# Seven block products for eight in the input projection of a convolution layer (fp32 network, one Trainium2 core)

## The chip, the cores and the metric

The kernel runs on one core of a Trainium2 chip. The metric is device microseconds of one execution; the time of a version is the median of several runs. The engines are TensorE (PE in the profile, with PEld for its weight loads), VectorE (DVE), ScalarE (ACT), GpSimd (POOL) and SyncE (SP), whose queue issues the DMAs.

## The reference

The network passes 1024 latent tokens of 1024 features, and 256 context tokens, through four layers: a pooling mixer, neighbourhood attention, a short gated convolution, and a pooling mixer again. The change is in the third. With `h` the RMS-normed, scaled and shifted tokens, it computes

```python
bg, cg, v, g = jnp.split(h @ w_in, 4, axis=-1)          # w_in: 1024 x 4096
y = bg * _dwconv3(cg * v, conv_w, conv_b)               # 3 taps over tokens, per feature
x = x + gate[:, None] * ((y * jax.nn.silu(g)) @ w_out)  # w_out: 1024 x 1024
```

All of it is fp32.

## The kernel before, in words

Activations lie transposed: features on the 128 partitions, tokens along the free dimension, in eight feature tiles (`KT`) and two token halves of 512 (`HALF`, called `ch` 0 and 1). A product keeps fp32 accuracy with fp32r matmuls: each operand is split into a high part (ACT, a copy to fp32r, L79) and a low part (DVE or POOL, source minus high part, L80), and `mm3` (to L117) issues three matmuls of 128x128 by 128x512 per contraction tile: high-high (L115), high-low (L116), low-high (L117). So one output tile of one token half (`gemm`, L133) is 8 x 3 = 24 matmuls into one PSUM bank; there are 8 banks.

The order of TensorE's instructions is the order of the program. On DVE, ACT, POOL and SP a planner orders the instructions ahead of time, by priority (place in the program) among those that its own timing takes to be ready; at run time each engine's queue is then strictly in that order. Tiles come from pools with a fixed number of buffers: `a` (`slot`, 33 tiles of 4 KB per partition) for activations, `raw` (3) for weights as loaded, `whi` and `wlo` (3 each) for their parts, `t2` (3 tiles of 2 KB) for temporaries. A tile's buffer is free when its last reader is done.

In `rest` (L1303) the attention layer's output projection (`out_proj`, L342) runs for token half 0 and then for half 1, with old residual rows loaded by `x1_rows` (L1019). Each finished half gives its sums of squares; `norm_later` (L281) hangs the normalisation on later gemms: the token sums on TensorE (L240), a chain of small DVE steps to the reciprocal root (L251 to L271), its spread over partitions on TensorE (L278), and `modulate_k` per feature tile (multiply by the spread in PSUM, L305; scale and shift for the high part, L306; the same again in fp32, L308 or L310; low part, L311).

`conv_in` (L1352) then loops over the 8 feature tiles of the output. For each it loads four weight tiles of 128x1024 (blocks cg, v, g, bg; `weight`, L82) and makes eight gemms, four blocks by two token halves. For the first tile the four gemms on half 0 come before those on half 1. ACT copies cg out of PSUM (L1369) and takes SiLU of g (L1373), DVE multiplies v by cg into `z` (L1371), then come three taps (L1390 to L1392), the product with bg straight from PSUM (L1395), with SiLU(g) on POOL (L1396), and the split for the next projection (L1398). `weight` also moves a background queue on: 24 reductions for the last layer's adaLN vector, each a 512 KB load into `raw` (L162) and one DVE reduction of 1024 columns (L166). Next is `out_proj` for `conv_out`, over the eight tiles of y, in SBUF.

## Time and profile before

| what | value |
|---|---|
| time, three runs | 1942.8, 1946.7 and 1949.32 us, median 1946.7 |
| profiled execution | 1943.86 us, span 1942.1 us |
| mean granted TensorE clock | 0.985 of full |
| TensorE busy | 1864.4 us (96%), 9936 matmuls |
| DVE, ACT, POOL busy | 1095.8 us (56%), 729.1 us (38%), 571.1 us (29%) |
| DMA | 274.21 MB, mean 141 GB/s |
| matmuls of `mm3` with loaded weights (L115) | x2160, 380 ns mean of one |

A matmul's recorded duration covers its whole passage and overlaps the next one's; the distance between two starts is what one costs in a row of them. Busy shares are averages over stages with different limits, so a stage is read from windows of its own. A releaser in brackets is the engine whose work ended the idle time named before it. All queues are in order, so an instruction that waits holds up what is behind it.

### The profile page before, as it was taken

What the parts mean: (1) busy time and instruction counts of PE and PEld (TensorE: products, weight loads), DVE (VectorE), ACT (ScalarE), POOL (GpSimd) and SP (SyncE); (2) the same over time, 40 slices, a digit from 0 to 9 for tenths busy, and PEclk for the clock granted to TensorE, in tenths of its full rate; (3) what the DMA queues carried; (4) which work ended last, traced back from release to release, by engine and by line L of the source; (5) the groups of instructions that cost most, each with busy time, mean ns of one, the idle gap of its engine ahead of it and who ended that gap; (6) DMA issues with size and microseconds to landing.
All of it is one profiled execution on the core that took longest, in us unless ns stands there. A gap on an engine that the chain in (4) does not pass through costs nothing.

```text
span 1942.1 us, 27112 instructions
## 1 busy us (share of the span) xinstructions
PE 1864.4 (96%) x9936; PEld 1604.0 (83%) x9936; DVE 1095.8 (56%) x2251; ACT 729.1 (38%) x1401; POOL 571.1 (29%) x552
## 2 busy tenths in 40 slices
PE   7888899999999999999998999999999999999997
PEld 4677778889998889999997877788888887888887
DVE  7989977256431066667666678544323346432627
ACT  3332215245122155666666555222212225322422
POOL 4645312652110033444433443100000024433120
PEclk9989999999999999999999999999999999999999
DMA  6233351554763466676677646443111165011234
GB/s 253 76 108 99 114 190 60 188 161 142 247 231 108 144 186 191 193 210 188 197 200 216 188 154 221 128 129 118 44 55 44 55 184 179 2 49 49 72 122 153
DMA packets 126960, 274.21 MB, mean 141 GB/s; under 512 B 12874, under 2 KB 48458, under 8 KB 126828
## 3 DMA queue, kind: packets, MB, share of 16 engines
q1 hardware_dynamic: 126828, 272.49, 44.9%
q8 instruction: 78, 1.28, 0.3%
q14 instruction: 54, 0.44, 0.1%
HBM read 218.63 MB, written 53.81 MB: 140 GB/s over the span
## 4 chain that ended last, share of the span: by engine, by line
PE 76%; DVE 12%; DMA 6%; issue 3%; POOL 2%; ACT 1%; SPq 0%; DVEq 0%; POOLq 0%; ACTq 0%
PE mm L117 22%; PE mm L115 21%; PE mm L116 21%; DVE junk L166 4%; PE T L1211 3%; PE O L1237 2%; PE O L1236 2%; DMA raw<-in_ada 2%; PE S L1154 1%; DVE S L455 1%; PE S L1155 1%; POOL S L455 1%; DMA a<-in_xT 1%; PE SC L1157 1%; PE SC L1156 1%
## 5 line engine op out<-in xcount | busy, mean ns | idle before, releaser
L115 PE MATMUL mm<-a,whi 128*128 128x512 f32 (+2 forms) x2160 | 819.9, 380 | 22.3 <-DVE U L418 10.0
L116 PE MATMUL mm<-a,whi 128*128 128x512 f32 (+2 forms) x2149 | 804.3, 374 | 10.9 <-DVE a L80 8.5
L117 PE MATMUL mm<-a,wlo 128*128 128x512 f32 (+2 forms) x2160 | 807.1, 374 | 3.5 <-POOL wlo L80 2.4
L115 PEld LDWEIGHTS mm<-a,whi 128*128 128x128 f32 x2160 | 411.5, 191 | 94.7 <-DVE U L418 11.3
L116 PEld LDWEIGHTS mm<-a,whi 128*128 128x128 f32 x2149 | 409.4, 190 | 81.0 <-DVE a L80 10.1
L117 PEld LDWEIGHTS mm<-a,wlo 128*128 128x128 f32 x2160 | 410.8, 190 | 77.9 <-POOL wlo L80 3.7
L80 POOL TENSOR_TENSOR wlo<-raw,whi 128x256 fp32r<-128x256 f32 (+2 forms) x150 | 191.0, 1288 | 382.5 <-ACT whi L79 341.9
L79 ACT ACTIVATE whi<-raw 128x1024 fp32r<-128x1024 f32 (+2 forms) x237 | 170.9, 738 | 352.1 <-PE mm L116 273.6
L166 DVE CUSTOM_DVE_ANT_0 junk<-raw,sil_x,vec 128x1024 bf16<-128x1024 f32 x86 | 117.9, 1371 | 94.4 <-DMA raw<-in_ada 94.1
L80 DVE TENSOR_TENSOR wlo<-raw,whi 128x1024 fp32r<-128x1024 f32 (+1 forms) x87 | 107.6, 1238 | 112.7 <-ACT whi L79 111.2
L1190 POOL TENSOR_SCALAR pr<-pr,rsum 128x640 f32<-128x640 f32 (+1 forms) x128 | 99.8, 779 | 238.8 <-DVE rsum L1189 188.2
L115 PE MATMUL mm<-a,a 128*128 128x512 f32 (+2 forms) x280 | 97.5, 348 | 7.4 <-ACT a L698 6.3
L1181 ACT ACTIVATE pr<-lg,nmx 128x640 f32<-128x640 f32 (+1 forms) x128 | 102.3, 799 | 2.6 <-DVE nmx L1171 1.6
L224 POOL TENSOR_TENSOR a<-a,a 128x512 f32<-128x512 f32 x42 | 59.9, 1425 | 144.2 <-ACT a L223 138.0
L116 PE MATMUL mm<-a,a 128*128 128x512 f32 (+2 forms) x275 | 95.8, 348 | 4.9 <-DVE a L702 4.9
L117 PE MATMUL mm<-a,a 128*128 128x512 f32 (+2 forms) x280 | 96.4, 344 | 0.5 <-DVE a L80 0.5
L1169 DVE TENSOR_SCALAR_CACHE_REDUCE lg<-SC 128x256 f32<-128x256 f32 x128 | 54.2, 423 | 72.9 <-PE SC L1157 72.8
L1220 DVE TENSOR_TENSOR ptlo<-T,pthi 128x512 fp32r<-128x512 f32 x128 | 88.2, 689 | 10.6 <-ACT pthi L1215 8.6
L1236 PE MATMUL O<-pthi,a 128*128 128x256 f32 x352 | 89.0, 286 | 3.2 <-ACT pthi L1215 3.2
L1237 PE MATMUL O<-ptlo,a 128*128 128x256 f32 x352 | 89.6, 289 | 1.1 <-DVE ptlo L1220 0.6
L1215 ACT ACTIVATE pthi<-T 128x512 fp32r<-128x512 f32 x128 | 76.4, 597 | 20.6 <-PE T L1211 19.5
L1211 PE MATMUL T<-ident,pr 128*128 128x128 f32 x512 | 77.6, 274 | 0.0
(182 smaller groups left out, 2495.0 us busy)
## 6 DMA issues: line engine op xcount, KB each, us to landing
raw<-in_ada SPq DMA_DIRECT2D x86, 512.0 KB
raw<-in_pool_out SPq DMA_DIRECT2D x32, 512.0 KB
raw<-in_conv_in SPq DMA_DIRECT2D x32, 512.0 KB
raw<-in_pool_in SPq DMA_DIRECT2D x27, 512.0 KB
x<-a SPq DMA_DIRECT2D x48, 256.0 KB
raw<-in_na_in SPq DMA_DIRECT2D x24, 512.0 KB
a<-dk SPq DMA_DIRECT2D x48, 256.0 KB
dv<-v SPq DMA_DIRECT2D x40, 256.0 KB
```

The costliest lines, as they stand in the source:

```text
L79: self.nc.scalar.activation(hi, src, AF.Copy)
L80: (lo_engine or self.nc.vector).tensor_tensor(lo, src, hi.bitcast(F32), op=ALU.subtract)
L115: t.matmul(ps, wh, hh, start=(begin and k == ks[0]), stop=False)
L116: t.matmul(ps, wh, hl, start=False, stop=False)
L117: t.matmul(ps, wl, hh, start=False, stop=(end and k == ks[-1]))
L166: nc.vector.tensor_tensor_reduce(out=junk[:], in0=raw[:], in1=self.sil[c][:], scale=1.0, scalar=self.vec[:, b:b + 1], op0=ALU.mult, op1=AL ...
L1181: nc.scalar.activation(pr[:, :L + CTX], lg[:, :L + CTX], AF.Exp, bias=nm[:], scale=-1.0, accum_out=sm[:])
L1190: nc.gpsimd.tensor_scalar(pr[:, :L], pr[:, :L], rs[:], 1.0, op0=ALU.mult, op1=ALU.mult)
L1211: nc.tensor.transpose(T[:, (s - b0) * P:(s - b0 + 1) * P], pr[:, o:o + P], self.ident[:])
L1220: nc.vector.tensor_tensor(lv, tv, hv.bitcast(F32), op=ALU.subtract)
L1236: nc.tensor.matmul(ops[:], v, hi[:, s, :], start=(n == 0), stop=False)
L1237: nc.tensor.matmul(ops[:], v, lo[:, s, :], start=False, stop=(n == len(seq) - 1))
```

## The change

Two weight tiles (128 output features each) form a pair: the z pair (cg, v) and the y pair (g, bg) of one feature tile, 16 pairs. In each, the weights are a 2x2 of blocks A (output tile by half of the contraction, four contraction tiles each), the tokens a 2x2 of blocks B (half of the contraction by token half). Eight block products of 12 matmuls become seven, with sums of weight blocks S1 to S4 and of token blocks T1 to T4 (`TERMS`). The products of a pair share three PSUM banks a, b, c: a takes products 1 and 2, b takes 6, 7 and 4, c takes 5 and 3; each bank is read in between and then added to again (`start` only for the first). The outputs are put together by DVE additions and ACT copies (`seven_after`).

The sums S are made per pair, on DVE for the first three pairs and on POOL from the fourth, where POOL also makes the low parts for products 1, 3 and 5. T1 to T4 and B22 are made once, in `conv_in`, from the kept fp32 tiles `x0` and `x1` of the two halves (`modulate_k` with `keep` works in place). The first three pairs are interleaved, so that their products 1 and 2, which need token half 0 alone, come first. Weight parts are made three products ahead. The adaLN reductions come one to every third product, from the fourth pair on.

The blocks B and T hold 28 of the 33 tiles of `a`, so seven of the eight tiles of y go to DRAM (`dyc`) and come back before `conv_out` (`conv_y`). `out_proj` takes the eighth last: for its first two output tiles it multiplies the other seven first (`late`). The second weight tile of a pair is loaded into `a`, the first into `raw`; `t2` has four buffers, and the pools of this stage (`pg`) and of the pooling layer (`pu`) are opened in turn.

```diff
-    def modulate_k(self, x, rs, l, c, k, hi, lo, n, pool=None, act=False):
+    def modulate_k(self, x, rs, l, c, k, hi, lo, n, pool=None, act=False, keep=False):
 ...
+        xh = x if keep else self.pt.tile([P, HALF], F32, tag="t2", name=self.nm("xh"), bufs=self.t2)[:, :n]
 ...
+            begun = {}
             for k in range(KT):
-                Wk = next(W)
+                if late is not None and group is groups[0] and k == 0:
+                    begun = {n: (next(W), self.bank()) for n in range(2)}
+                    for Wk, ps in begun.values():
+                        self.mm3(ps[:], self.wk(Wk), lambda q: y[group[0]][q], [q for q in order if q != late], end=False)
+                Wk = begun[k][0] if k in begun else next(W)
                 for ch in group:
                     g = self.gate(l, "c" if ch == "c" else "x")
                     old = xold(ch, k)
-                    ps = self.gemm(Wk, y, ch, ks.get((ch, k), order))
+                    if k in begun:
+                        ps = begun[k][1][:]
+                        self.mm3(ps, self.wk(Wk), lambda q: y[ch][q], (late,), begin=False)
+                        self.tick()
+                    else:
+                        ps = self.gemm(Wk, y, ch, ks.get((ch, k), order))
 ...
+        last = self.conv_in(h, x32, st)
         self.finish_background()
         h = {}
-        for ch, xn, st in self.out_proj(i["conv_out"], y, 2, ((0,), (1,)), self.old_from(self.x2), self.x3):
+        for ch, xn, st in self.out_proj(i["conv_out"], self.conv_y(last), 2, ((0,), (1,)), self.old_from(self.x2), self.x3, late=KT - 1):
 ...
+    TERMS = {1: ("A11", "B11"), 2: ("A12", "B21"), 3: ("S4", "B22"), 4: ("A22", "T4"), 5: ("S1", "T1"),
+             6: ("S2", "T2"), 7: ("S3", "T3")}
+    H4 = KT // 2
 ...
+            a, b, op = {"S1": ("A21", "A22", ALU.add), "S2": ("S1", "A11", ALU.subtract),
+                        "S3": ("A11", "A21", ALU.subtract), "S4": ("A12", "S2", ALU.subtract)}[name]
+            a, b = self.seven_block(pair, a), self.seven_block(pair, b)
+            t = self.pt.tile([P, HALF], F32, tag="t2", name=self.nm("s"), bufs=self.t2)
+            (self.nc.gpsimd if pair["pool"] else self.nc.vector).tensor_tensor(t[:], a, b, op=op)
+            pair["sums"][name] = t[:]
 ...
+    def seven_weight(self, pair, n):
+
+        src = self.seven_block(pair, self.TERMS[n][0])
+        self.ring = not self.ring
+        t = self.pw.tile([P, 2, HALF], F32R, tag="whi" if self.ring else "wlo", name=self.nm("wp"))
+        on_pool = pair["pool"] and n in (1, 3, 5)
+        self.split(t[:, 0], t[:, 1], src, self.nc.gpsimd if on_pool else None)
+        pair["parts"][n] = t
 ...
+    def seven_product(self, pair, n, T):
+        nc = self.nc
+        bank = "abc"[{1: 0, 2: 0, 6: 1, 7: 1, 4: 1, 5: 2, 3: 2}[n]]
+        first = n in (1, 6, 5)
+        if first:
+            pair[bank] = self.bank()
+        ps = pair[bank][:]
+        t = pair["parts"].pop(n)
+        B = T[self.TERMS[n][1]]
+        for q in range(self.H4):
+            s = slice(q * P, (q + 1) * P)
+            for i, (w, x) in enumerate(((0, 0), (0, 1), (1, 0))):
+                nc.tensor.matmul(ps, t[:, w, s], B[q][x], start=first and q == 0 and i == 0,
+                                 stop=q == self.H4 - 1 and i == 2, skip_group_check=True)
 ...
+        if n == 1:
+            pair["xu"] = self.pg.tile([P, 2, HALF], F32, tag="g", name=self.nm("xu"))
+            nc.scalar.activation(pair["xu"][:, 0], a[:], AF.Copy)
+        elif n == 2:
+            put(1, 0, a[:])
+        elif n == 6:
+            nc.vector.tensor_tensor(pair["xu"][:, 1], b[:], pair["xu"][:, 0], op=ALU.add)
+        elif n == 5:
+            if "ux" in pair:
+                u = pair["ux"][:, 1]
+                nc.vector.tensor_tensor(u, c[:], u, op=ALU.add)
+                put(2, 1, u)
+            else:
+                pair["ux"] = self.pg.tile([P, 2, HALF], F32, tag="g", name=self.nm("ux"))
+                nc.scalar.activation(pair["ux"][:, 0], c[:], AF.Copy)
+        elif n == 3:
+            u = pair["xu"][:, 1]
+            nc.vector.tensor_tensor(u, c[:], u, op=ALU.add)
+            put(1, 1, u)
+        elif n == 7:
+            before = "ux" in pair
+            if not before:
+                pair["ux"] = self.pg.tile([P, 2, HALF], F32, tag="g", name=self.nm("ux"))
+            u = pair["ux"]
+            nc.vector.tensor_tensor(u[:, 1], b[:], pair["xu"][:, 0], op=ALU.add)
+            if before:
+                nc.vector.tensor_tensor(u[:, 1], u[:, 1], u[:, 0], op=ALU.add)
+                put(2, 1, u[:, 1])
+        elif n == 4:
+            x = pair["xu"][:, 0]
+            nc.vector.tensor_tensor(x, b[:], x, op=ALU.add)
+            put(2, 0, x)
 ...
+        for j, (p, n) in enumerate(order):
+            while done < min(j + ahead + 1, len(order)):
+                q, m = order[done]
+                self.seven_weight(pairs[q], m)
+                done += 1
+            for f in hooks.get(j, ()):
+                f()
+            self.seven_product(pairs[p], n, T)
+            self.seven_after(pairs[p], n)
 ...
+                t = self.slot([P, 2, HALF], F32R)
+                nc.sync.dma_start(t[:].bitcast(F32), self.dyc[k][ch].bitcast(F32))
 ...
+        def first():
+            for k in range(H4):
+                self.modulate_k(x1[k], got[1], 2, "x", k, None, None, HALF, act=k % 2, keep=True)
+                sub(x0[k], x1[k], x0[k], False)
+                parts("T1", k, x0[k], k % 2)
+
+        def second():
+            for k in range(H4, KT):
+                self.modulate_k(x1[k], got[1], 2, "x", k, *parts("B22", k, None, None), HALF, k % 2, act=k % 2, keep=True)
+
+        def third():
+            for k in range(H4):
+                sub(x0[k], x1[k + H4], x0[k], k % 2)
+                parts("T2", k, x0[k], k % 2 == 0)
+            for k in range(H4):
+                sub(x1[k], x1[k + H4], x1[k], k % 2)
+                parts("T3", k, x1[k], k % 2 == 0)
+            for k in range(H4):
+                sub(x0[k + H4], x0[k + H4], x0[k], k % 2)
+                parts("T4", k, x0[k + H4], k % 2 == 0)
 ...
+        E = 3
+        order = [(p, 1) for p in range(E)] + [(p, 2) for p in range(E)]
+        for p in range(E):
+            order += [(p, n) for n in (5, 6, 3, 7)]
+            if p:
+                order.insert(-3, (p - 1, 4))
+        for p in range(E, len(pairs)):
+            end = p == len(pairs) - 1
+            steps = [(p, n) for n in ((1, 6, 2, 7, 5, 4, 3) if end else (1, 6, 5, 2, 7, 3, 4))]
+            if p == E:
+                steps.insert(1, (E - 1, 4))
+            order += steps
+        for p in pairs:
+            p["pool"] = True
+        for p in range(E):
+            pairs[p]["pool"] = False
+        hooks = {1: [tokens], 3: [spread, first], 4: [second], 5: [third]}
+        self.bg = [self.ada_all(3, (0, 1, 2))]
+        self.bg_rate = 0
+        for j in range(7 * E + 6, 7 * len(pairs) - 14, 3):
+            hooks.setdefault(j, []).append(lambda: self.background(1))
+        self.seven_run(pairs, T, order, hooks)
 ...
+                nc.vector.tensor_tensor(z[0][:, 1 + ch * HALF:1 + (ch + 1) * HALF], cs[1, ch], cs[2, ch], op=ALU.mult)
 ...
+            if ("g", ch) in cs and ("b", ch) in cs:
+                cv = cs["cv"]
+                nc.vector.tensor_tensor(cv[:, s], cs["b", ch], cv[:, s], op=ALU.mult)
                 t = self.slot([P, 2, HALF], F32R)
                 self.split(t[:, 0, :], t[:, 1, :], cv[:, s])
-                yp[ch].append((t[:, 0, :], t[:, 1, :]))
-        return yp
+                if k == KT - 1:
+                    last[ch] = (t[:, 0, :], t[:, 1, :])
+                else:
+                    nc.sync.dma_start(self.dyc[k][ch].bitcast(F32), t[:].bitcast(F32))
 ...
+        pair((1, 2), put_z)
+        pair((3, 0), put_y)
```

## Rows read from the trace of the kernel before

**Rows 1.** The page: span, busy times, the chain that ended last by engine.

```profile
span 1942.1 us, 27112 instructions
...
PE 1864.4 (96%) x9936; PEld 1604.0 (83%) x9936; DVE 1095.8 (56%) x2251; ACT 729.1 (38%) x1401; POOL 571.1 (29%) x552
...
PE 76%; DVE 12%; DMA 6%; issue 3%; POOL 2%; ACT 1%; SPq 0%; DVEq 0%; POOLq 0%; ACTq 0%
```

**Rows 2.** Timeline of TensorE: start us, us, engine, line, operation, shapes, count.

```profile
1188.30 0.39 PE L115 MATMUL mm<-a,whi 128*128 128x512 f32 x1
...
1300.04 0.39 PE L115 MATMUL mm<-a,whi 128*128 128x512 f32 x1
...
1301.40 0.39 PE L115 MATMUL mm<-a,whi 128*128 128x512 f32 x1
...
1546.88 0.39 PE L115 MATMUL mm<-a,whi 128*128 128x512 f32 x1
```

**Rows 3.** Windows: us; PE, PEld, DVE, ACT, POOL busy; granted clock; DMA share; GB/s.

```profile
1188.30:1226.00 37.70, 33.42 (x138) 26.32 (x137) 32.71 (x54) 21.01 (x28) 8.88 (x6) 0.91 0.52 174
1226.00:1387.00 161.00, 161.00 (x712) 133.35 (x711) 66.68 (x84) 32.76 (x42) 11.71 (x16) 1.00 0.35 109
1387.00:1546.90 159.90, 159.90 (x708) 132.43 (x707) 45.59 (x44) 31.45 (x40) 9.61 (x15) 1.00 0.15 50
```

**Rows 4.** Timeline of TensorE at the stage start; in brackets idle, releaser.

```profile
1196.94 1.87 PE L240 MATMUL mm<-ones,a 128*128 128x1 f32 x8 [2.19 <-DVE a L227]
1198.67 0.77 PE L115 MATMUL mm<-a,a 128*128 128x512 f32 x1
...
1203.08 0.40 PE L116 MATMUL mm<-a,a 128*128 128x512 f32 x1
...
1206.30 1.05 PE L278 MATMUL mm<-a,ones 128*128 128x128 f32 x8
...
1224.19 0.50 PE L116 MATMUL mm<-a,whi 128*128 128x512 f32 x1 [1.33 <-DVE a L311]
```

**Rows 5.** Groups of DVE, 1189 to 1547 us: count, busy, mean ns, idle.

```profile
L166 DVE CUSTOM_DVE_ANT_0 junk<-raw,sil_x,vec 128x1024 bf16<-128x1024 f32 x24 | 32.4, 1351 | 49.9 <-DMA raw<-in_ada 49.8
...
L1395 DVE TENSOR_TENSOR a<-mm,a 128x512 f32<-128x512 f32 x15 | 10.4, 691 | 26.3 <-PE mm L117 26.3
L80 DVE TENSOR_TENSOR a<-a,a 128x512 fp32r<-128x512 f32 x15 | 10.3, 687 | 14.5 <-ACT a L79 14.5
...
L1391 DVE SCALAR_TENSOR_TENSOR a<-z,vec,a 128x1024 f32<-128x1024 f32 x8 | 10.3, 1282 | 25.6 <-ACT a L1390 25.6
```

**Rows 6.** One line of POOL, whole run: count, ns min/median/max, first, last.

```profile
L1396 POOL TENSOR_TENSOR a<-a,a x16: 1282/1291/2137, 1238.4 to 1547.9; 128x512 f32<-128x512 f32 x16
```

**Rows 7.** Timeline of DVE where POOL is busy too, columns as in rows 2.

```profile
1165.60 1.22 DVE L80 TENSOR_TENSOR wlo<-raw,whi 128x1024 fp32r<-128x1024 f32 x1
1166.73 1.28 DVE L305 TENSOR_TENSOR xh<-a,mm 128x512 f32<-128x512 f32 x2
...
1547.94 2.34 DVE L80 TENSOR_TENSOR wlo<-raw,whi 128x1024 fp32r<-128x1024 f32 x1 [0.17 <-ACT whi L79]
```

**Rows 8.** Timeline of POOL in the same two places.

```profile
1165.56 2.40 POOL L224 TENSOR_TENSOR a<-a,a 128x512 f32<-128x512 f32 x1 [7.21 <-ACT a L223]
...
1547.91 1.29 POOL L1396 TENSOR_TENSOR a<-a,a 128x512 f32<-128x512 f32 x1 [4.15 <-ACT whi L79]
```

**Rows 9.** Groups of ACT, 1189 to 1547 us, columns as in rows 5.

```profile
L1390 ACT ACTIVATE a<-z,vec 128x1024 f32<-128x1024 f32 x8 | 9.9, 1238 | 7.6 <-DVE z L1371 7.6
L79 ACT ACTIVATE a<-a 128x512 fp32r<-128x512 f32 x15 | 9.5, 632 | 72.4 <-POOL a L1396 72.4
```

**Rows 10.** Timeline of DVE at the end of the last feature tile.

```profile
1541.64 0.69 DVE L1395 TENSOR_TENSOR a<-mm,a 128x512 f32<-128x512 f32 x1 [3.35 <-PE mm L117]
1544.46 0.69 DVE L80 TENSOR_TENSOR a<-a,a 128x512 fp32r<-128x512 f32 x1 [2.13 <-ACT a L79]
```

**Rows 11.** Waits, 1189 to 1547 us: us in total, times, longest us.

```profile
DVE junk L166 <- DMA raw<-in_ada: 49.8, 18, 4.3
```

More of the change, by code (lines that the diff above doesn't have):

```diff
@@ L7 @@
+import contextlib
 import itertools
@@ L303, in modulate_k @@
         A, B = A[:, k:k + 1], m[:, k:k + 1]
[L304 removed]
+        xh = x if keep else self.pt.tile([P, HALF], F32, tag="t2", name=self.nm("xh"), bufs=self.t2)[:, :n]
         nc.vector.tensor_tensor(xh, x, rs, op=ALU.mult)
[L306 removed]
+        if hi is not None:
+            nc.scalar.activation(hi, xh, AF.Identity, bias=B, scale=A)
         if act:
@@ L339, in stats, with out_proj @@
         return st
-    def out_proj(self, wsrc, y, l, groups, xold, spill, order=range(KT), ks={}):
+    def out_proj(self, wsrc, y, l, groups, xold, spill, order=range(KT), ks={}, late=None):
         nc = self.nc
@@ L614, in scratch @@
         self.dy = [d.tile([P, SEQ], F32, name=f"dy{h}") for h in range(HEADS // 2)]
+        self.dyc = [[d.tile([P, 2, HALF], F32R, name=f"dyc{k}_{ch}") for ch in range(2)] for k in range(KT - 1)]
         self.dmask = d.tile([2, MROWS, SEQ], F32R, name="dmask")
@@ new lines, in seven_after @@
+    def seven_after(self, pair, n):
+        nc, put = self.nc, pair["put"]
+        a, b, c = (pair.get(x) for x in "abc")
+        if n == 1:
[30 more added lines that the diff above has]
+            put(2, 0, x)
@@ new lines, in seven_run, with conv_y @@
+    def seven_run(self, pairs, T, order, hooks, ahead=3):
+        self.ring = False
+        done = 0
+        for j, (p, n) in enumerate(order):
[7 more added lines that the diff above has]
+            self.seven_after(pairs[p], n)
+    def conv_y(self, last):
+        nc = self.nc
+        y = {0: [], 1: []}
+        for ch in (0, 1):
+            for k in range(KT - 1):
+                t = self.slot([P, 2, HALF], F32R)
+                nc.sync.dma_start(t[:].bitcast(F32), self.dyc[k][ch].bitcast(F32))
+                y[ch].append((t[:, 0, :], t[:, 1, :]))
+            y[ch].append(last[ch])
+        return y
@@ new lines, in conv_in, with parts, tokens, spread @@
+    def conv_in(self, h, x32, st):
+        nc, i = self.nc, self.i
+        H4 = self.H4
+        if 0 not in h:
+            self.flush()
+        h0, x0, x1 = h[0], x32[0], x32[1]
+        T = {"B11": h0[:H4], "B21": h0[H4:]}
+        got = []
+        def parts(name, k, src, pool):
+            if k % H4 == 0:
+                T[name] = []
+            t = self.slot([P, 2, HALF], F32R)
+            T[name].append((t[:, 0, :], t[:, 1, :]))
+            if src is not None:
+                self.split(t[:, 0, :], t[:, 1, :], src, nc.gpsimd if pool else None)
+            return T[name][-1]
+        def tokens():
+            got.append(self.rstd_tokens(st))
+        def spread():
+            got.append(self.rstd_spread(*got[0]))
+        def sub(out, a, b, pool):
+            (nc.gpsimd if pool else nc.vector).tensor_tensor(out, a, b, op=ALU.subtract)
+        def first():
[16 more added lines that the diff above has]
+                parts("T4", k, x0[k + H4], k % 2 == 0)
+        pairs, last = [], {}
+        for k in range(KT):
+            self.conv_pairs(k, pairs, last)
+        E = 3
[20 more added lines that the diff above has]
+        self.seven_run(pairs, T, order, hooks)
+        self.conv_close()
+        return last
@@ new lines, in conv_pairs, with pair, put_z, gated @@
+    def conv_pairs(self, k, pairs, last):
+        nc, i = self.nc, self.i
+        z, cs = [], {}
+        def pair(rows, put):
+            pairs.append(dict(src=[i["conv_in"][r * KT + k] for r in rows], raw={}, sums={}, parts={}, put=put))
+        def put_z(row, ch, v):
+            if not z:
+                z.append(self.pg.tile([P, SEQ + 2], F32, tag="z", name=self.nm("z"), bufs=1))
+                nc.gpsimd.memset(z[0][:, 0:1], 0.0)
+                nc.gpsimd.memset(z[0][:, SEQ + 1:SEQ + 2], 0.0)
+            cs[row, ch] = v
+            if (3 - row, ch) in cs:
+                nc.vector.tensor_tensor(z[0][:, 1 + ch * HALF:1 + (ch + 1) * HALF], cs[1, ch], cs[2, ch], op=ALU.mult)
+            if all((r, c) in cs for r in (1, 2) for c in (0, 1)):
+                for key in [x for x in cs if isinstance(x, tuple) and x[0] in (1, 2)]:
+                    del cs[key]
+                cv = cs["cv"] = self.pg.tile([P, SEQ], F32, tag="g", name=self.nm("cv"))
+                tap = lambda t: self.vec[:, V_CW + 8 * t + k:V_CW + 8 * t + k + 1]
+                nc.scalar.activation(cv[:], z[0][:, 1:1 + SEQ], AF.Identity, bias=self.vec[:, V_CB + k:V_CB + k + 1], scale=tap(1))
+                nc.vector.scalar_tensor_tensor(cv[:], z[0][:, 0:SEQ], tap(0), cv[:], op0=ALU.mult, op1=ALU.add)
+                nc.vector.scalar_tensor_tensor(cv[:], z[0][:, 2:2 + SEQ], tap(2), cv[:], op0=ALU.mult, op1=ALU.add)
+                for c in waiting:
+                    gated(c)
+        waiting = []
+        def gated(ch):
+            s = slice(ch * HALF, (ch + 1) * HALF)
+            nc.gpsimd.tensor_tensor(cs["cv"][:, s], cs["cv"][:, s], cs["sg"][:, s], op=ALU.mult)
+        def put_y(row, ch, v):
+            s = slice(ch * HALF, (ch + 1) * HALF)
+            if row == 1:
+                if "sg" not in cs:
+                    cs["sg"] = self.slot([P, SEQ])
+                nc.scalar.activation(cs["sg"][:, s], v, AF.Silu)
+                if "cv" in cs:
+                    gated(ch)
+                else:
+                    waiting.append(ch)
+                cs["g", ch] = True
+            else:
+                cs["b", ch] = v
+            if ("g", ch) in cs and ("b", ch) in cs:
+                cv = cs["cv"]
+                nc.vector.tensor_tensor(cv[:, s], cs["b", ch], cv[:, s], op=ALU.mult)
```

89 lines of the change are left out of this document (36 added, 53 removed).

## The prediction

> **What bounds the kernel now.** The page first: TensorE is busy for 96% of the span and carries 76% of the chain that ended last, with VectorE (DVE) next at 12% [rows 1]. A busy TensorE is not yet a bound, so the stage of the change is cut out by windows. The input projection of the convolution layer starts its first matmul at 1188.30 us and the next layer step (conv_out) starts at 1546.88 us [rows 2]: 358.6 us. In it TensorE has no idle time after 1226 us, at granted clock 1.00, while DVE, ScalarE (ACT) and GpSimd (POOL) are at 41% and less, DVE in the first half the highest with 66.7 of 161 us, and the DMA engines at 35% and then 15% [rows 3]. The spacing of matmuls is the price of one: six starts from 1300.04 to 1301.40 us, 0.2267 us each [rows 2]. (Their recorded 0.39 us overlap; that is not the price.) The stage has 8 feature tiles x 4 blocks x 2 token halves x 24 = 1536 matmuls, 348.2 us. The remaining 10.4 us are all in the first 38 us: TensorE waits for the sum of squares of the second token half until 1196.94, runs ten matmuls in 4.41 us instead of 2.27 after that (0.43 us each, the 1.2 GHz level, in a stretch of granted clock 0.91), and waits for the second half's normalised tiles at 1224.19 [rows 3, 4]. So this stage is bound by the number of matmuls, and little else.
>
> **What the change takes away.** A pair of output tiles took 8 products of 12 matmuls and takes 7: 84 for 96. There are 16 pairs: 192 matmuls fewer, at 0.2267 us **43.5 us**. They were issued back to back, so nothing hides that saving. By the sustained spacing of 131 ns that the Trainium skill gives for 512 columns (TensorE: Matmul & The Clock Gate, Back-to-back issue gap) it would be 25.2 us; the trace's 0.2267 us at full granted clock disagrees and decides.
>
> **What it adds to the other engines.** Weights: 112 parts of 512 columns for 32 of 1024, thus more work in all, and four sums of blocks per pair. Outputs: five evictions per pair on DVE with adds, two copies on ACT. Tokens: sixteen tiles T1 to T4, by subtraction and split. DVE's 512-column operations cost 0.69 us and its 1024-column ones 1.28 [rows 5], POOL's of 512 columns 1.29 [rows 6]. What matters is that DVE and POOL do not run these side by side. At 1547.94 a DVE subtraction of two SBUF tiles took 2.34 us instead of 1.22 while a POOL one of 1.29 us ran from 1547.91; at 1165.56 it was POOL's that took 2.40, while DVE's ran its 1.22. DVE's multiplications with a PSUM operand at 1166.73 ran through the POOL operation at 0.64 us each [rows 7, 8]. So two-SBUF operations of both engines add up, those with a PSUM operand do not.
>
> Per pair after the third (sums on POOL): POOL has 4 sums, 3 low parts and 1 gate product, 8 x 1.29 = 10.3 us. DVE has, two-SBUF, 4 low parts, 1 add, half of 5 gate, z and split operations (7.5 x 0.69 = 5.2), half of two taps (1.28), together 6.5 us; and 7/3 adaLN reductions of 1.28 us [rows 5] in ten of the pairs, 3.0 us. That is 19.8 us in turn against 84 x 0.2267 = 19.0 us of TensorE. DVE's four PSUM evictions and half a z product, 3.1 us, can run beside POOL. ACT has 7 x 0.63 for high parts [rows 9], two copies, and half of the gates and taps: under 8 us, covered.
>
> So where the reductions run I take 0.8 us per pair over, but some of it is cover by three products of lookahead: **7 us** over ten pairs. Bounds: nothing, if short overlaps at the ends make up the 0.8 us; 38 us, if DVE never finds a PSUM operation to put beside POOL: its own 12.6 us plus 10.3 is 22.9, 3.8 over per pair. I take the near end, since in the present trace the loser of a collision waits no longer than the holder's operation. In the six other pairs the load is 16.8 of 19.0: nothing.
>
> **The start.** Now four blocks on the first token half, 96 matmuls or 21.8 us, cover the normalisation of the second. After, only six products (A11 B11 and A12 B21 of three pairs, 72 matmuls, 16.3 us) lie ahead of T1, and then T2, B22, T3 and T4 are wanted within five more. The sums of squares are ready at 1196.9 as now; TensorE has by then done one product for one block of 24, so it waits 2.7 us longer. 24 matmuls later the spread of the norm ends at 1207.4 [rows 4], as now. From there until T4: DVE 4 scale-and-shift steps, 10 subtractions, 10 low parts, and for weights and sums of the products some 6 more, 30 x 0.64 [rows 7] = 19.2 us; POOL 6 subtractions and 10 low parts, 16 x 1.29 = 20.6 us [rows 6]. In turn 39.8 us: 1247.8 after the first multiplication (0.6). The product with T4 is the twelfth; it ends about 1248.5 where unbroken matmuls from 1188.30 would end at 1220.9. Lost 27.6 for 10.4 now: **17 us given back**. Bounds: 2 us, if the engines overlapped and POOL's 20.6 us alone decided (1211 to 1232); 26, if in addition the stalls bring the lower clock level twice more (2.1 us each, [rows 4]) and the kept first-half tiles delay the last loads of the step before by 5 us.
>
> **The end.** Seven of eight output tiles are stored and loaded again: 14 stores and 14 loads of 512 KB on SP's queue, behind and ahead of weight loads, where DMA is at 15% [rows 3]. Loads for the first half can begin when the last pair's first product frees tiles; 7 x 0.524 MB at 174 GB/s [rows 3] take 21 us, and 72 matmuls cover 16.3. The late eighth tile has 42 matmuls (9.5 us) of cover; its chain took 1541.64 to 1545.15 = 3.5 us [rows 10]. I take **2 us** (0 to 8). What waits on SP behind a store is the next weight load; three products of lookahead (8.2 us) hide it.
>
> **A new wait that has to be priced.** Three PSUM banks per pair are added to again after they are read, so TensorE now waits for evictions that it passed by before. The tightest is product 4 behind the reading of product 7, one product (2.72 us) between, 0.69 us to do: 2.0 us to spare. DVE's queue sat still for its adaLN loads 18 times, 49.8 us in all, longest 4.3 [rows 11], and evictions queue behind that. It costs nothing today; here some of it shows. It lies within the 0 to 38 us above.
>
> **Sum:** 43.5 - 17 - 7 - 2 = 17.5 us. The profiled execution took 1943.9 us (span 1942.1, [rows 1]), 2.8 below the median of 1946.7, so 1926.4 in its terms and **1929 us** as a median.
>
> **Rivals.** *Full saving.* If the planner lays POOL's work into DVE's gaps and fills the start with later weights, only 2 + 0 + 2 come back, 39.5 us: 1907. For it: DVE was idle for most of the stage. Against it: the collisions. *Slower: DVE and POOL in turn become the bound of every pair.* If DVE stands behind each POOL operation, pairs take 22.9 us and TensorE sees it at the re-read banks: 43.5 - 17 - 38 - 2 = -13.5, 1960 us. It decides from 3.1 us lost per pair, 22.1 us a pair. Against it, evictions from PSUM can pass. A rule of the Trainium skill says just this: the pair of ports that DVE and GpSimd share is locked for a whole instruction and the loser blocks fully (SBUF — State Buffer, Who interferes with whom); the trace agrees on two-SBUF operations, and the PSUM rows agree with its exception. *A wash.* With 26 at the start and 1.2 us per pair, 43.5 - 26 - 12 - 2 = 3.5: 1943. That the product count does not fall is no case: 84 for 96 stands in the loops.
>
> **Chances.** A run tells 0.3% (5.8 us) from no change: below 1940.9 is faster, above 1952.5 slower. Forecast (1913 to 1940) 0.50; full saving 0.22; a wash 0.14; slower 0.14. Faster 0.72, same 0.14, slower 0.14. The range, 1907 to 1950, leaves out the slow case and little of the best.
>
> **What would show it.** Matmuls 9936 to 9744. Right: the stage after 1188 us is 341 us long rather than 358.6; TensorE waits for split tiles and POOL until some 1248, then only small gaps; DVE and POOL operations stretched where they meet. Steps wrong: T4's product ending well before 1248 or after 1255; pairs of 19.0 (no price) or above 22 us (the slow rival); a gap over 5 us ahead of conv_out, with loads late. The forecast as a whole is wrong if TensorE waits for PSUM readers in every pair, or if nothing is lost beyond the first 20 us.

## The result, and the profile after

The changed kernel takes 1966.7 us, median of four runs (1966.3 to 1967.3), against 1946.2 for the kernel before beside it (four runs, 1942.8 to 1949.3): ratio 1.0106, 95% interval 1.0088 to 1.0123. It is slower by 20.4 us; 1929 was predicted, in a range of 1907 to 1950.

The page of the kernel after, the lines that answer to [rows 1]:

```profile
span 1964.5 us, 27237 instructions
...
PE 1841.1 (94%) x9744; PEld 1575.3 (80%) x9744; DVE 1231.9 (63%) x2400; ACT 777.1 (40%) x1508; POOL 741.6 (38%) x655
...
PE 63%; DVE 17%; DMA 7%; POOL 5%; issue 4%; ACT 2%; SPq 1%; DVEq 0%; POOLq 0%; ACTq 0%
```

The 192 matmuls are gone (9936 to 9744). What grew is DVE by 136 us and POOL by 171 us of busy time, and in the chain TensorE fell from 76% to 63% while DVE and POOL rose from 14% to 22%.

Windows over the stage of the kernel after (columns as in [rows 3]): from its first matmul to the start of the 145th, which ends the first twelve products; from there to the end of the last (0.2267 us after its start); then to the first matmul of conv_out. Below them, the seventy products from the 29th to the 98th, where 20 of the 24 adaLN reductions run, and the fourteen after; then one z pair and the y pair behind it, out of the seventy.

```profile
1189.14:1250.00 60.86, 40.55 (x162) 30.89 (x161) 50.36 (x77) 28.20 (x47) 31.22 (x18) 0.83 0.15 48
1250.00:1556.70 306.70, 283.37 (x1201) 229.20 (x1199) 224.14 (x249) 102.33 (x162) 167.96 (x120) 0.97 0.34 119
1556.70:1563.80 7.10, 0.20 (x1) 0.01 (x1) 3.52 (x5) 1.26 (x2) 1.85 (x7) 0.78 0.53 196
...
1297.80:1518.20 220.40, 200.93 (x842) 162.18 (x841) 159.15 (x174) 73.51 (x119) 130.82 (x94) 0.96 0.35 120
1518.20:1556.70 38.50, 38.32 (x169) 31.25 (x167) 27.46 (x29) 13.87 (x21) 17.98 (x12) 1.00 0.35 123
...
1343.32:1367.68 24.36, 21.26 (x86) 16.78 (x84) 20.50 (x22) 7.11 (x13) 16.89 (x10) 0.93 0.44 151
1367.68:1386.72 19.04, 19.04 (x86) 15.77 (x84) 12.05 (x16) 7.13 (x11) 9.27 (x9) 1.00 0.34 111
```

Read each length against unbroken matmuls at 0.2267 us [rows 2]. The first twelve products should take 144 x 0.2267 = 32.6 us: 28.2 lost. The other hundred should take 272.0: 34.8 lost, with the bounds unrounded (1249.95 to 1556.74). Then 7.1 us pass without work. The stage is 374.7 us long where it was 358.6. The seventy products should take 190.4 us: 30.0 of the 34.8 are lost there, and the last two pairs lose only 0.6. So most of the loss sits where the reductions are; whether they cause it alone is for the experiments. It is not spread evenly: the five z pairs of the seventy products take 22.6 to 28.0 us, the five y pairs between them 19.0, which is full speed, and the y pairs too have reductions (two each in four of them).

The five longest waits of TensorE in the stage of the kernel after (us in total, times, longest), and below them what L1451 has of it within the seventy products:

```profile
PE mm L1438 <- DVE xu L1451: 14.2, 7, 2.6
PE mm L1438 <- POOL a L81: 11.2, 2, 10.7
PE mm L116 <- DMA a<-dyc: 6.9, 1, 6.9
PE mm L1438 <- ACT xu L1447: 6.2, 4, 2.9
PE mm L1438 <- ACT a L80: 5.7, 1, 5.7
...
PE mm L1438 <- DVE xu L1451: 13.1, 5, 2.6
```

L1451 is DVE's eviction of product 6, L1447 ACT's copy of product 1; both free a bank that a later product adds to. The POOL and ACT rows are the T blocks of the start, the DMA row is the end. What makes the eviction late is seen in one z pair. Timelines of DVE, then POOL, then TensorE in the kernel after:

```profile
1353.12 2.32 DVE L167 CUSTOM_DVE_ANT_0 junk<-raw,sil_x,vec 128x1024 bf16<-128x1024 f32 x1
...
1355.36 1.75 DVE L81 TENSOR_TENSOR wp<-a,wp 128x512 fp32r<-128x512 f32 x1
1357.03 0.68 DVE L1451 TENSOR_TENSOR xu<-mm,xu 128x512 f32<-128x512 f32 x1
...
1352.72 1.63 POOL L1413 TENSOR_TENSOR s<-s,raw 128x512 f32<-128x512 f32 x1
1354.31 2.25 POOL L1413 TENSOR_TENSOR s<-raw,a 128x512 f32<-128x512 f32 x1
1356.52 1.72 POOL L81 TENSOR_TENSOR wp<-raw,wp 128x512 fp32r<-128x512 f32 x1
...
1357.76 0.50 PE L1438 MATMUL mm<-a,wp 128*128 128x512 f32 x1 [2.63 <-DVE xu L1451]
```

A reduction (1.28 us where POOL has no sums, in sums_on_dve below) and a low part (0.69) take 2.32 and 1.75 us beside POOL's sums. The ends of these five operations alternate between the engines, POOL 1354.35, DVE 1355.44, POOL 1356.56, DVE 1357.11, POOL 1358.24, each a little less than its own length alone after the one before: they go in turn. The eviction behind them in DVE's queue is itself untouched at 0.68 us, but starts only at 1357.03, and TensorE has then waited 2.63 us. The same over the hundred products, groups of DVE and POOL:

```profile
L167 DVE CUSTOM_DVE_ANT_0 junk<-raw,sil_x,vec 128x1024 bf16<-128x1024 f32 x24 | 42.6, 1774 | 9.0 <-DMA raw<-in_ada 8.9
L81 DVE TENSOR_TENSOR wp<-s,wp 128x512 fp32r<-128x512 f32 x30 | 34.9, 1164 | 18.4 <-ACT wp L80 18.0
...
L1451 DVE TENSOR_TENSOR xu<-mm,xu 128x512 f32<-128x512 f32 x15 | 10.2, 681 | 0.0
...
L1413 POOL TENSOR_TENSOR s<-raw,s 128x512 f32<-128x512 f32 x13 | 22.5, 1732 | 0.0
```

The reductions mean 1774 ns against 1351 [rows 5], a low part 1164 against 687 [rows 5], a sum on POOL 1732 against 1291 [rows 6]; the evictions with a PSUM operand stay at 681. DVE sits still for adaLN loads 8.9 us where it was 49.8 [rows 11].

### The profile page after: what moved, and what is told of

It is laid out like the page before. It is cut to its first block, busy times and chain, and to the rows that moved or that the text cites. A ratio compares the mean times of both kernels' runs of the same rounds, so it can differ in the third digit from the quotient of the medians.

```text
span 1964.5 us, 27237 instructions
## 1 busy us (share of the span) xinstructions
PE 1841.1 (94%) x9744; PEld 1575.3 (80%) x9744; DVE 1231.9 (63%) x2400; ACT 777.1 (40%) x1508; POOL 741.6 (38%) x655
## 4 chain that ended last, share of the span: by engine, by line
PE 63%; DVE 17%; DMA 7%; POOL 5%; issue 4%; ACT 2%; SPq 1%; DVEq 0%; POOLq 0%; ACTq 0%
PE mm L118 16%; PE mm L116 16%; PE mm L117 16%; PE mm L1438 5%; DVE junk L167 5%; PE T L1230 2%; PE O L1256 2%; DMA raw<-in_ada 2%; POOL s L1413 2%; PE O L1255 2%; DMA a<-in_conv_in 1%; DVE wp L81 1%; PE S L1173 1%; DVE S L471 1%; POOL S L471 1%
## 5 line engine op out<-in xcount | busy, mean ns | idle before, releaser
L116 PE MATMUL mm<-a,whi 128*128 128x512 f32 (+2 forms) x1696 | 641.6, 378 | 30.2 <-DVE U L434 9.9
L117 PE MATMUL mm<-a,whi 128*128 128x512 f32 (+2 forms) x1685 | 624.7, 371 | 7.0 <-DVE a L81 6.8
L118 PE MATMUL mm<-a,wlo 128*128 128x512 f32 (+2 forms) x1696 | 627.9, 370 | 3.1 <-POOL wlo L81 2.2
L116 PEld LDWEIGHTS mm<-a,whi 128*128 128x128 f32 x1696 | 325.0, 192 | 86.8 <-DVE U L434 11.2
L118 PEld LDWEIGHTS mm<-a,wlo 128*128 128x128 f32 x1696 | 324.4, 191 | 59.9 <-POOL wlo L81 3.8
L117 PEld LDWEIGHTS mm<-a,whi 128*128 128x128 f32 x1685 | 323.3, 192 | 58.3 <-DVE a L81 8.5
L1438 PE MATMUL mm<-a,wp 128*128 128x512 f32 x1344 | 322.6, 401 | 41.6 <-DVE xu L1451 14.2
L1438 PEld LDWEIGHTS mm<-a,wp 128*128 128x128 f32 x1344 | 258.4, 194 | 104.8 <-DVE xu L1451 17.1
L81 POOL TENSOR_TENSOR wlo<-raw,whi 128x256 fp32r<-128x256 f32 (+2 forms) x150 | 190.4, 1284 | 384.7 <-ACT whi L80 357.7
L80 ACT ACTIVATE whi<-raw 128x256 fp32r<-128x256 f32 (+2 forms) x208 | 140.0, 693 | 226.2 <-PE mm L117 168.4
L167 DVE CUSTOM_DVE_ANT_0 junk<-raw,sil_x,vec 128x1024 bf16<-128x1024 f32 x86 | 130.7, 1519 | 49.5 <-DMA raw<-in_ada 48.9
L81 DVE TENSOR_TENSOR wlo<-raw,whi 128x1024 fp32r<-128x1024 f32 (+1 forms) x58 | 66.7, 1152 | 80.3 <-ACT whi L80 78.5
L116 PE MATMUL mm<-a,a 128*128 128x256 f32 (+2 forms) x232 | 78.7, 339 | 8.2 <-ACT a L717 6.3
L1234 ACT ACTIVATE pthi<-T 128x512 fp32r<-128x512 f32 x128 | 76.3, 596 | 20.4 <-PE T L1230 19.1
L117 PE MATMUL mm<-a,a 128*128 128x256 f32 (+2 forms) x227 | 77.1, 340 | 3.3 <-DVE a L721 3.0
```

Of the source, the lines that this page charges most:

```text
L80: self.nc.scalar.activation(hi, src, AF.Copy)
L81: (lo_engine or self.nc.vector).tensor_tensor(lo, src, hi.bitcast(F32), op=ALU.subtract)
L116: t.matmul(ps, wh, hh, start=(begin and k == ks[0]), stop=False)
L117: t.matmul(ps, wh, hl, start=False, stop=False)
L118: t.matmul(ps, wl, hh, start=False, stop=(end and k == ks[-1]))
L167: nc.vector.tensor_tensor_reduce(out=junk[:], in0=raw[:], in1=self.sil[c][:], scale=1.0, scalar=self.vec[:, b:b + 1], op0=ALU.mult, op1=AL ...
```

## The experiments

Three theories on the 34.8 us. A: DVE and POOL take turns at operations that read two SBUF tiles, and their in-order queues hand the delay on to the evictions. B: the adaLN reductions stand ahead of evictions in DVE's queue. C: re-reading a PSUM bank costs a wait however the queues are filled. "Start", "steady" and "end" below are the losses of the three windows above, worked out in the same way for each kernel from the start of its first and 145th matmul, the end of its last and the first matmul of conv_out; the time is of one run, or the median where the text names one. Executions of one kernel differ by some 6 us (1942.8 to 1949.3 before), and the kernels entered the stage between 1188.0 and 1194.8 us, so the losses carry the argument and small differences of the times do not.

| kernel | time, us | start | steady | end |
|---|---|---|---|---|
| the change | 1966.7 | 28.2 | 34.8 | 7.1 |
| sums_on_dve | 1940.1 | 30.0 | 6.1 | 7.0 |
| no_adaln | 1939.4 | 26.0 | 6.9 | 7.2 |
| sums_on_dve_no_adaln | 1932.7 | 25.8 | 0.0 | 7.0 |
| all_on_dve | 1931.1 | 23.7 | 5.3 | 7.0 |
| pool_reads_added | 1988.4 | 26.7 | 53.6 | 7.0 |
| pool_writes_added | 1935.3 | 25.1 | 4.0 | 7.0 |
| dyc_loads_on_act | 1938.5 | 21.8 | 6.0 | 8.6 |
| best_guess | 1937.8 | 17.4 | 1.0 | 10.6 |
| all_on_dve_timed | 1932.6 | 22.0 | 4.4 | 7.0 |
| t_blocks_apart | 1928.4 | 16.9 | 0.8 | 7.0 |
| stored_tiles_early | 1913.5 | 17.1 | 2.2 | 0.0 |

### Sums on DVE, reductions left out, and both

**sums_on_dve** gives DVE the pairs' sums and low parts that the change gives to POOL:

```diff
         for p in pairs:
-            p["pool"] = True
+            p["pool"] = False
```

> The four weight sums and the low parts of products 1, 3 and 5 of every pair are made on DVE; POOL keeps the gate product and its share of the token blocks. The changed kernel takes 1966.7 us; after the block T4 it needs 308 us for its last 100 products (272 us unbroken), a loss of 36 us. Theory A (DVE and POOL take turns at two-SBUF operations, and each engine's queue carries the delay on to the PSUM evictions): DVE's own work is then some 16 to 17 us of the 19 us of a pair, with hardly a collision, so the loss falls from 36 to under 12 us and the time to 1937 to 1945. Theory B (the adaLN reductions stand ahead of the evictions in DVE's queue): DVE gets more to do and the reductions stay, so the loss stays at 30 us or more, 1960 to 1975. Theory C (a PSUM bank that is added to after it was read costs a wait however the queues are filled): loss 25 to 40, 1955 to 1970.

**no_adaln** leaves out the last layer's adaLN loads and reductions (constants stand for what they give):

```diff
-        self.bg = [self.ada_all(3, (0, 1, 2))]
+        nc.vector.memset(self.AB[3, "x"][1][:], 0.0)
+        nc.vector.memset(self.AB[3, "x"][0][:], 1.0)
+        self.bg = []
```

> As the changed kernel, but the 24 adaLN loads and reductions of the last layer are left out (its scale and shift are set by constants, so that part of the computation is missing). Theory A: turns of DVE and POOL fall from 19.8 to 16.8 us per pair, collisions stay in all other operations: the loss of 36 us falls to 12 to 22 us, 1943 to 1953. Theory B: nearly all of it goes, under 8 us left, 1935 to 1940. Theory C: unchanged within 8 us, 1958 to 1967.

**sums_on_dve_no_adaln** makes both edits.

> Both: sums and low parts on DVE, and the adaLN loads and reductions left out. Theory A: loss under 6 us, 1932 to 1938, little below the version with sums on DVE alone. Theory B: under 6 us too, but then far below the version with sums on DVE alone (20 us or more). Theory C: 20 us or more of loss stays, 1952 or more.

Measured 1940.1, 1939.4 and 1932.7 us. The seventy products of the first (in its trace 1298.00 to 1493.20) and of the second (1298.40 to 1491.20), and the hundred products of the third, as windows:

```profile
1298.00:1493.20 195.20, 191.69 (x841) 157.26 (x840) 157.68 (x246) 71.52 (x118) 17.30 (x21) 1.00 0.40 136
```

```profile
1298.40:1491.20 192.80, 191.94 (x842) 157.26 (x841) 128.31 (x131) 71.59 (x116) 118.95 (x91) 1.00 0.22 82
```

```profile
1249.20:1521.30 272.10, 272.10 (x1201) 224.98 (x1199) 198.69 (x291) 103.57 (x162) 23.52 (x29) 1.00 0.25 88
```

The third falsifies C: 1200 matmuls in 272.1 us, not one wait, with the banks re-read as before. The first has the telling line. DVE now does all the sums and low parts as well, 246 instructions instead of 174, and is busy for 157.68 us where it was busy for 159.15: in the changed kernel the 73 instructions that POOL has more (94 against 21) took as much of DVE's time in collisions as they took off its hands. B alone falls here, since the reductions are still there and all but 4.8 us of the 30.0 have gone. A's band held for this kernel. But no_adaln came out where B put it (1935 to 1940, under 8 us left; 6.9 were) and not in A's 1943 to 1953, so A alone does not give the sizes either. Either relief is enough: the loss needs POOL's share and the reductions together. The prediction's mean count of turns fits that, 19.8 us a pair with the reductions and 16.8 without, against 19.0 of TensorE.

**all_on_dve** also gives DVE the T blocks, B22 and their low parts.

```diff
-                parts("T1", k, x0[k], k % 2)
+                parts("T1", k, x0[k], False)
...
-                sub(x0[k], x1[k + H4], x0[k], k % 2)
-                parts("T2", k, x0[k], k % 2 == 0)
+                sub(x0[k], x1[k + H4], x0[k], False)
+                parts("T2", k, x0[k], False)
...
```

> Sums and low parts on DVE as in the first, and the token blocks T1 to T4 and B22 too: POOL has only the gate products. Theory A for the start: 46 DVE operations of 0.60 to 0.64 us in a row take 28 to 30 us instead of 40 in turn, the twelfth product ends near 1238 instead of 1249 us and 8 to 12 us come back on top of the first version: 1927 to 1936. If the start is bound by the latency of the chain from norm to T4 rather than by turns, it changes by less than 4 us. If the end (7 us of waiting for the loads of y) is all that is left, the stage loses about 20 us there and at the start.

Measured 1931.1. The start loses 23.7 us with POOL idle, less than the 28.2 with its help. The twelfth product, expected to end near 1238 us, ended at 1244.4. Three windows of the start, and a wait of TensorE in it:

```profile
1202.00:1212.00 10.00, 10.00 (x45) 8.07 (x43) 10.00 (x18) 5.29 (x9) 0.00 (x0) 1.00 0.00 0
1212.00:1222.00 10.00, 2.56 (x6) 1.33 (x6) 10.00 (x18) 8.21 (x13) 0.00 (x0) 0.78 0.00 1
1222.00:1232.00 10.00, 6.23 (x22) 4.52 (x21) 10.00 (x18) 5.18 (x10) 0.00 (x0) 0.84 0.06 13
...
PE mm L1438 <- DVE xu L1451: 6.3, 1, 6.3
```

DVE is busy for 10.00 of each 10.00 us, so most of this is work. But TensorE also waited 6.3 us once for L1451, product 6's eviction queued behind T3 and T4; that is taken up below.

### Only POOL added: with reads, and with writes alone

To test A without touching the kernel's own work, sums_on_dve gets POOL instructions whose result nobody needs, seven a pair. **pool_reads_added**:

```diff
         pair["parts"][n] = t
+        if pair["idle"]:
+            self.nc.gpsimd.tensor_tensor(self.scr[:], src, src, op=ALU.add)
...
```

> All sums and low parts of the pairs on DVE as in sums_on_dve, plus seven POOL additions a pair (from the fourth pair on), each reading a product's 512-column weight tile twice and writing a scratch tile that nobody reads. No instruction of the kernel waits for them other than through the weight tiles' buffers. Theory A (DVE and POOL take turns at two-operand instructions on SBUF): 7 x 1.29 = 9 us of POOL beside some 14 us of two-operand work on DVE give 23 us a pair against 19.0 of PE, so DVE falls behind again as in the changed kernel: 1955 to 2010 us. If the order of the queues alone made the loss: unchanged, 1936 to 1946.

**pool_writes_added** has a memset in its place, ahead of the split that fills the tile:

```diff
+        if pair["idle"]:
+            self.nc.gpsimd.memset(t[:].bitcast(F32), 0.0)
...
```

> As sums_on_dve, plus seven POOL memsets a pair of the low part's tile ahead of the instruction that fills it: POOL work that reads nothing, and that the fill has to wait for. Theory A holds the turns to instructions with two operands in SBUF: the steady loss stays near 6 us, 1936 to 1948 us. If any POOL work beside DVE costs as much as an addition, or if the longer chain to each low part matters: over 1955 us.

Measured 1988.4 and 1935.3 us, 48.3 more and 4.8 less than sums_on_dve (the 4.8 is within the scatter). Groups of the hundred products, first with reads added, with TensorE's two longest waits there, then with writes, then sums_on_dve itself:

```profile
L1426 POOL TENSOR_TENSOR scr<-s 128x512 bf16<-128x512 f32 x52 | 71.7, 1379 | 78.7 <-DVE s L1413 76.6
...
L81 DVE TENSOR_TENSOR wp<-s,wp 128x512 fp32r<-128x512 f32 x58 | 59.7, 1031 | 0.1
...
PE mm L1440 <- DVE ux L1471: 21.3, 6, 4.7
PE mm L1440 <- DVE xu L1453: 9.4, 6, 3.0
```

```profile
L1424 POOL MEMSET wp<- 128x1024 f32 x91 | 86.9, 956 | 121.5 <-PE mm L1440 96.3 <-issue 22.9 <-DVE s L1413 1.7
...
L81 DVE TENSOR_TENSOR wp<-s,wp 128x512 fp32r<-128x512 f32 x56 | 38.7, 695 | 1.5 <-ACT wp L80 1.5
```

```profile
L81 DVE TENSOR_TENSOR wp<-s,wp 128x512 fp32r<-128x512 f32 x56 | 38.1, 682 | 0.2
```

The same DVE instruction takes 1031, 695 and 682 ns. 87 us of POOL work that only writes costs nothing. Additions that read lengthen the two-SBUF operations of DVE that they meet (the reductions from 1281 to 1576 ns, too; DVE's taps, and two of its four sums, stay as they were), and TensorE waits for DVE's evictions (21.3 us for product 7's, L1471, and 9.4 for product 6's, L1453). Two other explanations fall by the same pair of traces. Over the hundred products DVE's 339 instructions, and ACT's 162, stand in the same order in pool_reads_added as in sums_on_dve, so it is not an order that the planner changed; and no listed wait of any engine is for one of the added additions, so it is not the buffers that they hold. That settles the turns of A. The Trainium skill says this too (SBUF — State Buffer, Who interferes with whom): a DVE instruction with two SBUF inputs contends with a GpSimd one that reads SBUF, not with one that only writes it. The runs agree, with 1031 against 695 ns.

### The start: T blocks at three places

**t_blocks_apart** is all_on_dve with T2, T3 and T4 built one at a time:

```diff
-        hooks = {1: [tokens], 3: [spread, first], 4: [second], 5: [third]}
+        hooks = {1: [tokens], 3: [spread, first], 4: [second], 5: [t2], 7: [t3], 9: [t4]}
...
```

> As all_on_dve, with T2, T3 and T4 built at three places of the order and not at one; the adaLN reductions and the loads of the stored tiles stay where the change has them. In best_guess the first twelve products lost 17.4 us against 23.7 in all_on_dve. If the place of T3 and T4 made that difference: loss 16 to 19 us here too, steady loss 5 to 6, end wait 7 as in all_on_dve, and about 6 us less than all_on_dve in the same call. If it came from the reductions that best_guess has moved away: start loss 22 to 24 us and the time of all_on_dve.

> The kernel of all_on_dve again, timed in rounds beside the two others: 1929 to 1940 us, since its single look gave 1931.1 and dyc_loads_on_act, whose input projection is the same, 1938.5, of which 6.8 us were lost before this projection began (it started at 1194.8 us against 1188.0).

**best_guess**, run before these two, had this edit with the loads of the next section on ACT and the reductions moved to conv_out:

> As dyc_loads_on_act, with two more steps. T2, T3 and T4 are built at three places of the order and not at one, so that the eviction of product 6 doesn't stand behind T3 and T4 on DVE (PE's wait of 6.3 us in all_on_dve): start loss from 23.7 to 16 to 20 us. The last layer's adaLN reductions are moved from this projection to the output projection: steady loss from 5.3 to under 1 us. By theory A both gain where DVE is the bound and nothing elsewhere: 1908 to 1918 us. If the reductions disturb the output projection as they did the input projection: 1918 to 1930 us.

t_blocks_apart measured 1928.4 us (median of four, ratio to before 0.9906, 0.9887 to 0.9926), all_on_dve_timed 1932.6 (0.9934, 0.9913 to 0.9955). The start loses 16.9 us against 22.0, and TensorE's wait for L1451 is gone, so the place of T3 and T4 made that difference. The steady loss, expected to stay at 5 to 6, fell as well, from 4.4 to 0.8 us, with the reductions in place: the waits for product 7's eviction (L1469) went from 2.9 us to 0.5. Why is open. best_guess at 1937.8 missed both its 1908 to 1918 and its 1918 to 1930: its start and steady losses came out at 17.4 and 1.0, but conv_out paid. A window there:

```profile
1512.50:1600.00 87.50, 70.59 (x285) 55.63 (x285) 51.22 (x80) 16.93 (x22) 11.99 (x14) 0.86 0.86 299
```

The adaLN loads now run beside conv_out's weights and the fourteen stored tiles, DMA at 0.86, and TensorE works 70.6 of 87.5 us. Which of the two moves cost what there, the reductions' or the loads', no run separates.

### The end: fourteen loads behind a weight load

Timeline of SP's queue, of DVE and of TensorE at the end of the stage of the kernel after:

```profile
1547.37 11.86 SPq L87 DMA_DIRECT2D raw<-in_conv_out  x3
1559.28 11.22 SPq L1499 DMA_DIRECT2D a<-dyc  x14
...
1557.62 1.22 DVE L81 TENSOR_TENSOR wlo<-raw,whi 128x1024 fp32r<-128x1024 f32 x1
...
1563.82 0.76 PE L116 MATMUL mm<-a,whi 128*128 128x512 f32 x1 [6.92 <-DMA a<-dyc]
```

The third of conv_out's weight loads needs a raw buffer that DVE's low part at 1557.62 sets free, and the fourteen loads of the stored tiles (L1499) stand behind it: they issue from 1559.28, 2.5 us after the last matmul. **dyc_loads_on_act** is all_on_dve with these loads on ACT's queue:

```diff
-                nc.sync.dma_start(t[:].bitcast(F32), self.dyc[k][ch].bitcast(F32))
+                nc.scalar.dma_start(t[:].bitcast(F32), self.dyc[k][ch].bitcast(F32))
```

> As all_on_dve (1931.1 us), with the fourteen loads that open the output projection issued by ACT and not by SP, where they stand behind the third weight load, which waits for a low part on DVE. If that queue made the wait of 7.0 us of PE at the first product of the output projection: wait under 2 us, 1922 to 1927 us. If the transfers themselves, or the stores that they read back, make it: the wait stays at 6 to 7 us, 1929 to 1933 us.

Measured 1938.5 us, and an end of 8.6: a miss (6.8 us of its 7.4 over all_on_dve were lost ahead of the stage). ACT's rows say why the end did not shrink:

```profile
1531.29 0.63 ACT L80 ACTIVATE a<-cv 128x512 fp32r<-128x512 f32 x1 [2.35 <-DVE cv L1629]
1531.35 8.64 ACTq L1499 DMA_DIRECT2D a<-dyc  x12
```

On ACT they stand behind the last tile's high part instead. The other queue was as full; what had to move was the place in the order. **stored_tiles_early** writes the loads into the last pair of t_blocks_apart, after the products that give up their blocks' tiles:

```diff
+        def load(ch, ks):
+            for k in ks:
+                t = self.slot([P, 2, HALF], F32R)
+                nc.sync.dma_start(t[:].bitcast(F32), self.dyc[k][ch].bitcast(F32))
+                self.yl[ch].append((t[:, 0, :], t[:, 1, :]))
...
+        hooks.setdefault(N - 5, []).append(lambda: load(0, range(0, 4)))
+        hooks.setdefault(N - 3, []).append(lambda: load(0, range(4, KT - 1)))
+        hooks.setdefault(N - 2, []).append(lambda: load(1, range(KT - 1)))
```

> As t_blocks_apart, with the fourteen loads of the stored tiles written into the last pair, where the products have given up their blocks' tiles, and not after it. If the order of the queues makes the end wait of 7 us: the loads are issued before the projection's last matmul, the wait is under 2 us, and the time 6 to 10 us under t_blocks_apart: 1915 to 1923 us. If the tiles come free too late or the loads stand behind others again: no gain, 1922 to 1928 us.

Measured 1913.5 us, median of four (1912.9 to 1916.7), against 1944.4 before: ratio 0.9839, 0.9823 to 0.9855. It beats both kernels. SP's queue and TensorE in it:

```profile
1482.60 3.90 SPq L1580 DMA_DIRECT2D a<-dyc  x4
...
1500.81 5.93 SPq L1580 DMA_DIRECT2D a<-dyc  x10
...
1511.79 2.43 PE L1438 MATMUL mm<-a,wp 128*128 128x512 f32 x10
1514.06 0.39 PE L116 MATMUL mm<-a,whi 128*128 128x512 f32 x1
```

All fourteen are issued before the stage ends and conv_out follows without a gap. The time lies below the expected 1915 to 1923: the gain over t_blocks_apart, 14.9 us between the medians, is more than the 7.0 of the gap. The 150 matmuls after it lost another 4.8 us there and none here. These two, less 1.4 us of steady loss, about cover the 9.7 us between the two profiled executions (1922.9 and 1913.2); the rest of the 14.9 is that t_blocks_apart's profiled execution was the fastest of its four. (all_on_dve and dyc_loads_on_act, alike up to here, entered the stage at 1188.0 and 1194.8.)

## Why the prediction was wrong

**The saving** was right: 192 matmuls, and 0.2267 us each, as sums_on_dve_no_adaln shows (272.1 us for 1200).

**The start** was right in size: the twelfth product was to end at 1248.5 and did at 1250.0; 17 us were to be given back, and 28.2 - 10.4 = 17.8 were. Its reason, DVE and POOL in turn, fits: TensorE's two long waits there (5.7 and 10.7 us) come at the first product that needs T2, the longer for a low part on POOL, and POOL's share was no help at all (28.2 with it, 23.7 and 22.0 without). That the size fits so closely has some luck in it: with everything on DVE the same kind of count gave 1238 for 1244.4, since it does not price the order: product 6's eviction stood behind T3 and T4 there, at a cost of 5.1 us (22.0 to 16.9). What that costs in the changed kernel, where no such wait is listed, no run shows.

**The adaLN zone** is the step that failed: "So where the reductions run I take 0.8 us per pair over", 7 us with bounds of 0 and 38, at the near end "since in the present trace the loser of a collision waits no longer than the holder's operation". The place was right, the size was 30.0 in the ten pairs (34.8 in all). Two things were wrong in it. The 0.8 us was a mean over z and y pairs, and the work does not fall evenly: in the z pair shown above the end of the tile before (L1629 and its splits on DVE, a gate product on POOL) comes on top, so that DVE is busy for 20.5 us and POOL for 16.9, against 12.1 and 9.3 in the y pair behind it. All of the 30.0 us is lost in the five z pairs; that this unevenness is the reason is read from the traces, not tested. And its rows were of single collisions. In a stream of them each operation of either engine is lengthened in turn (rows of L167, L81 and L1413 above), DVE gains no time by what it gives away, and an eviction that could run beside POOL stands in DVE's in-order queue behind one that can't. On average a pair took 22.0 us, at the point (22.1) from which the slower rival was said to decide: this rival, with its 38 us over the ten pairs, 1960 us and a chance of 0.14, was nearest to what happened, though not in every pair, as it had it, but in every second. The rule of the Trainium skill that stood beside that rival (SBUF — State Buffer, Who interferes with whom) bore on the case more than the exception that was taken against it: the evictions do pass POOL, as 681 ns shows, but only once they are at the head of DVE's queue.

**The end** was taken as 2 us with bounds of 0 to 8, "Loads for the first half can begin when the last pair's first product frees tiles". The tiles were free early enough, as stored_tiles_early shows; the queue was not. The price was 7.1 us of wait and, by the spacing of the next 150 matmuls, 3.7 more.

**The new wait** was there, but not at the product named: not at product 4 behind the reading of 7, but at 7 behind 6 (L1451) and 2 behind 1 (L1447). The one named (L1469) cost 2.8 us once in the changed kernel, and it is the only wait left in the hundred products of all_on_dve (3.7 us in five).

The sum with measured terms: 43.5 - 17.8 - 34.8 - 10.8 = -19.9 us; measured -20.4 between the medians. The spans of the two profiled executions differ by 22.4, of which 0.8 lies ahead of the stage and some 1.7 behind the next 150 matmuls; the sum leaves these out.

## What to carry to other kernels

Before giving DVE's work to POOL, count what both read from SBUF in turn: an operation of 0.69 us on DVE that becomes one of 1.29 on POOL costs more of what they share than it frees, unless DVE has PSUM work to put beside it and that work isn't queued behind the rest. Count it for each stretch in which the work falls and not as a mean over unlike ones. Where a change re-reads PSUM banks, list what stands ahead of each eviction in its engine's queue. A load that is to be early must be early in the order of its queue, and another queue helps only if it stands better there.
